# Chunks of 68, 60, 60 and 68 rows instead of four of 64, and the last store in two parts, in a DMA-bound matrix product

## The chip, the cores and the metric

The kernel runs on one core of a Trainium2 chip. The metric is the device time of one execution, in microseconds (us). Every execution also has a record of its span, from the core's first to its last instruction.

Ratios of two kernels are the mean time of one kernel's runs over that of the other's runs of the same rounds on the same chip, with a 95% interval. They are therefore not quite the ratio of the medians that are quoted beside them.

## The reference

```python
def reference(x, W, lora_A, lora_B, lora_E, scale):
    x_flat = x.reshape(-1, 256)                 # x: 16 x 2048 x 256, so 32768 rows of 1 KB
    y = x_flat @ W                              # W: 256 x 256
    lora_out = ((x_flat @ lora_A) * lora_E) @ lora_B    # rank 16
    return (y + scale * lora_out).reshape(16, 2048, 256)
```

All of it is float32. 33.55 MB are read and 33.55 MB are written. The kernel folds the low-rank part into one bfloat16 weight of 256 x 256, so each row needs one multiplication.

## The kernel before

The 32,768 rows are cut into four chunks of 64 rows per partition. Partition `p` of chunk `c` holds 64 consecutive rows, so neighbouring partitions lie 64 KB apart in memory. Three chunks fit in SBUF, the core's own memory (the "homes"); results overwrite their inputs and are stored from there; chunk 3 takes the home of chunk 0 once that is stored. One queue, on the sync engine (SP), issues all loads and stores in this order:

```python
ROWS = 64
N_CHUNKS = 4
N_HOMES = 3
ORDER = [                    # L: load, S: store; chunk, first row, last row
    ("A",),
    ("L", 0, 0, 8), ("L", 0, 8, 24), ("L", 0, 24, 40), ("L", 0, 40, 64),
    ("L", 1, 0, 32), ("L", 1, 32, 64),
    ("L", 2, 0, 16), ("L", 2, 16, 64),
    ("S", 0, 0, 40), ("S", 0, 40, 64),
    ("L", 3, 0, 32), ("L", 3, 32, 64),
    ("S", 1, 0, 64), ("S", 2, 0, 64), ("S", 3, 0, 64),
]                            # (set here with several entries to a line)
HELD = (2, 16)
HOLDERS = (("S", 0, 0, 40),)
# ... cut ...
    x_chunks = x_flat.rearrange("(c p b) k -> c p b k", p=P, b=ROWS)
    y_chunks = out_flat.rearrange("(c p b) m -> c p b m", p=P, b=ROWS)
# ... cut: in sync_program, for each entry (kind, c, s, e) of ORDER ...
            if kind == "L":
                for st in stored:
                    if st[1] == c - N_HOMES and st[2] < e and s < st[3]:
                        sync.wait_ge(stored[st], 16)
                ins = sync.dma_start(out=at_home, in_=x_chunks[c, :, s:e, :]).then_inc(loaded[op], 16)
            else:
                sync.wait_ge(s_done, ends.index((c * ROWS + e) // CG - 1) + 1)
                sync.dma_start(out=y_chunks[c, :, s:e, :], in_=at_home).then_inc(stored.get(op, stored_rest), 16)
```

Rows are computed in 64 groups of four rows per partition. The cast to bfloat16 is on POOL (GpSimd), the transposes and multiplications on PE (TensorE; PEld is its loading of weights), one copy on DVE (VectorE) and the copy of the result back to its home on ACT (ScalarE). POOL is held at row 16 of chunk 2 until the first store has landed.

## Time and profile before

| | before |
|---|---|
| time, median of 3 runs | 161.51 us (161.44 to 161.85) |
| execution whose profile is shown here | span 161.5 us, time 162.84 us |
| DMA queue of loads and stores, share of 16 engines' span | 97.2% |
| last instruction that computes ends | 118.6 us |

These lines are from the page of the kernel before: busy time (and share) of the engines; a row of 40 equal slices, each digit the busy share of the mean DMA engine in tenths; the DMA queue of loads and stores, q1, and a small one named instruction, q14 (packets, MB, share of 16 engines); and the chain that ended last.

```profile
span 161.5 us, 2024 instructions
...
PE 95.4 (59%) x782; PEld 83.4 (52%) x782; DVE 45.4 (28%) x66; ACT 66.1 (41%) x65; POOL 66.9 (41%) x70
...
DMA  7999999999999997998999999799799799699690
...
q1 hardware_dynamic: 2304, 67.13, 97.2%
...
q14 instruction: 3, 0.02, 0.0%
...
DMA 36%; PE 34%; POOL 1%; ACT 1%; issue 0%; SPq 0%; ACTq 0%; POOLq 0%
```

The DMA engines hardly rest, and no other engine is near that. The chain's share of PE (34%) does not contradict it: the chain passes through the engine that released the last issue, and that store then stood in a queue behind others.

When the loads and stores were issued shows in SP's timeline of the kernel before (start, length of the piece in us, operation, count):

```profile
0.43 4.95 SPq L148 DMA_DIRECT2D home<-in_x_dram  x8
27.66 9.87 SPq L153 DMA_DIRECT2D out_dram<-home  x2
75.94 7.69 SPq L148 DMA_DIRECT2D home<-in_x_dram  x2
83.68 35.34 SPq L153 DMA_DIRECT2D out_dram<-home  x3
```

The last store is issued by 119 us; queued stores keep the engines busy for 42 us more.

Two stretches of the kernel before, by windows (columns: from and to, length, busy time of PE, PEld, DVE, ACT and POOL, granted clock, DMA share, GB/s):

```profile
24.00:40.00 16.00, 14.52 (x134) 13.29 (x133) 7.61 (x11) 11.10 (x11) 11.78 (x12) 1.00 0.99 428
50.00:66.00 16.00, 10.96 (x101) 9.94 (x98) 5.87 (x9) 9.33 (x10) 6.97 (x7) 0.95 0.98 403
```

From 50 to 66 us the engines move less although they are as busy. Here the first store follows the loads of chunks 0 to 2.

Finally, the trace has a record of each DMA packet: start, duration, size. One packet is one partition's piece of one transfer, so each transfer is 128 packets, eight to an engine. The records do not name the engine; packets are chained here by the start of one falling on the end of another, within a few ns. The "excess" of a packet is its duration less that of the fastest packet of its size in the same trace.

```
packets of the kernel before (from the trace's records)
size B    count   fastest us   median us   longest us
 8192      128      0.309        0.309       0.754
49152      128      1.815        1.820       2.718
65536      384      2.418        2.418       2.625
excess summed over all packets, divided by 16 engines: 1.58 us
  of it in packets starting at  0 to 16 us: 0.49    56 to 64 us: 0.83    96 to 104 us: 0.09
one engine, eight packets in a row from 100.68 to 121.21 us: 2.516 to 2.625 us each instead of 2.418
```

### The profile page before, as it was taken

Reading aid. Unit: us, or ns where it says so; the run is one execution under the profiler, and the core shown is the slowest. Engines: PE = TensorE matmul, PEld = TensorE weight load, DVE = VectorE, ACT = ScalarE, POOL = GpSimd, SP = SyncE. Lnnn points to the kernel's source line nnn. Section 1 sums busy time; section 2 is a strip of 40 time slices with the busy share of each in tenths; the row PEclk is TensorE's granted clock in tenths of the full one; section 3 lists DMA queues with packets and bytes.
Section 4 is the critical chain, followed back from the end, with each engine's and each line's share of the span. In section 5 each row is a group of like instructions: output and inputs, shape, how many; then the busy total and the mean of one; then the engine's idle time right before and its main releaser. Section 6 shows DMA issues by size and latency. Waiting matters only on the chain.

```text
span 161.5 us, 2024 instructions
## 1 busy us (share of the span) xinstructions
PE 95.4 (59%) x782; PEld 83.4 (52%) x782; DVE 45.4 (28%) x66; ACT 66.1 (41%) x65; POOL 66.9 (41%) x70
## 2 busy tenths in 40 slices
PE   2988999969999990000899999999910000000000
PEld 1347999959999990000789989999900000000000
DVE  0141555535555550000155555555400000000000
ACT  3003677747777772000157777777730000000000
POOL 1516768577778840001578777788200000000000
PEclk9975999999999999555599999999996555555555
DMA  7999999999999997998999999799799799699690
GB/s 253 405 438 452 402 452 446 446 406 446 394 548 414 402 390 337 477 467 371 420 459 440 406 446 536 319 519 471 308 503 487 308 503 503 292 503 503 292 519 16
DMA packets 2515, 67.43 MB, mean 418 GB/s; under 512 B 448, under 2 KB 464, under 8 KB 592
## 3 DMA queue, kind: packets, MB, share of 16 engines
q1 hardware_dynamic: 2304, 67.13, 97.2%
q10 hardware_dynamic: 208, 0.28, 0.6%
q14 instruction: 3, 0.02, 0.0%
HBM read 33.85 MB, written 33.55 MB: 417 GB/s over the span
## 4 chain that ended last, share of the span: by engine, by line
DMA 36%; PE 34%; POOL 1%; ACT 1%; issue 0%; SPq 0%; ACTq 0%; POOLq 0%
DMA out_dram<-home 30%; PE psum_y L237 22%; PE psum_xt L226 12%; DMA home<-in_x_dram 6%; POOL stage L177 1%; ACT home L193 1%; ACTq L195 0%; SPq L308 0%; POOLq L176 0%; SPq L272 0%
## 5 line engine op out<-in xcount | busy, mean ns | idle before, releaser
L193 ACT COPY home<-psum_y 128x1024 f32<-128x1024 f32 x64 | 64.8, 1012 | 50.5 <-PE psum_y L237 50.5
L177 POOL CAST stage<-home 128x1024 bf16<-128x1024 f32 x64 | 66.2, 1042 | 44.8 <-DMA out_dram<-home 17.5
L237 PE MATMUL psum_y<-weff,xt 128*128 128x256 bf16 x512 | 69.6, 281 | 0.0
L210 DVE COPY xt<-psum_xt 128x1024 bf16<-128x1024 bf16 x64 | 44.3, 692 | 63.4 <-PE psum_xt L226 63.4
L237 PEld LDWEIGHTS psum_y<-weff,xt 128*128 128x128 bf16 x512 | 51.8, 101 | 6.5
L226 PE MATMUL psum_xt<-ident,stage 128*128 128x128 f32 x260 | 41.4, 283 | 19.3 <-POOL stage L177 19.0
L226 PEld LDWEIGHTS psum_xt<-ident,stage 128*128 128x128 f32 x260 | 31.5, 146 | 22.1 <-issue 20.7
L250 PE MATMUL psum_y<-ident 128*128 128x512 f32 x4 | 3.7, 1078 | 2.9 <-POOL ident L158 2.9
L250 PEld LDWEIGHTS psum_y<-ident 128*128 128x128 f32 x4 | 1.2, 324 | 3.9 <-POOL ident L158 2.9
L200 DVE TENSOR_SCALAR ate<-psum_y,e_sb 16x256 f32<-16x256 f32 x1 | 0.5, 472 | 6.9 <-PE psum_y L253 6.9
L193 ACT ACT_TABLE_LOAD x1 | 1.3, 1283 | 2.1 <-SPq L272 2.1
L259 PE MATMUL psum_y<-b_sb,ate 16*128 16x256 f32 x4 | 1.1, 400 | 0.0
L156 POOL MEMSET ident<- 128x128 f32 x1 | 0.2, 205 | 1.7 <-SPq L272 1.7
L253 PEld LDWEIGHTS psum_y<-ident,a_sb 128*16 128x16 f32 x2 | 0.2, 114 | 1.2 <-issue 1.2
L214 DVE TENSOR_TENSOR weff<-w_sb,psum_y 128x512 bf16<-128x512 f32 x1 | 0.7, 687 | 0.4 <-PE psum_y L259 0.4
L259 PEld LDWEIGHTS psum_y<-b_sb,ate 16*128 16x128 f32 x4 | 0.7, 184 | 0.2 <-issue 0.2
L158 POOL TENSOR_SCALAR_AFFINE_SELECT ident<-ident 128x128 f32<-128x128 f32 x1 | 0.3, 293 | 0.2 <-POOL ident L156 0.2
L253 PE MATMUL psum_y<-ident,a_sb 128*16 128x128 f32 x2 | 0.4, 273 | 0.0
L294 POOL MEMSET const-float32-0.0<- 128x1 f32 x1 | 0.1, 99 | 0.2 <-issue 0.2
L294 POOL MEMSET const-bfloat16-1.0<- 128x1 bf16 x1 | 0.1, 103 | 0.0
L294 POOL MEMSET const-uint8-127<- 128x1 uint8 x1 | 0.1, 103 | 0.0
L294 POOL MEMSET const-float32-1.0<- 128x1 f32 x1 | 0.1, 99 | 0.0
## 6 DMA issues: line engine op xcount, KB each, us to landing
home<-in_x_dram SPq DMA_DIRECT2D x4, 4096.0 KB, 25.1
home<-in_x_dram SPq DMA_DIRECT2D x3, 2048.0 KB, 13.8
home<-in_x_dram SPq DMA_DIRECT2D x1, 6144.0 KB, 58.9
out_dram<-home SPq DMA_DIRECT2D x1, 5120.0 KB, 48.3
home<-in_x_dram SPq DMA_DIRECT2D x1, 3072.0 KB, 20.7
out_dram<-home SPq DMA_DIRECT2D x1, 3072.0 KB, 46.0
home<-in_x_dram SPq DMA_DIRECT2D x1, 1024.0 KB, 5.4
w_sb<-in_W_dram ACTq DMA_DIRECT2D x1, 256.0 KB, 3.0
```

What stands on the lines that cost most here:

```text
L158: gpsimd.affine_select(out=ident[:], in_=ident[:], compare_op=ALU.not_equal, fill=1.0, base=0, pattern=[[-1, P]], channel_multiplier=1,).t ...
L177: gpsimd.tensor_copy(out=stage[g % NS][:], in_=home(c)[:, b:b + CG, :]).then_inc(s_stage[g % UNROLL], 1)
L193: scalar.copy(out=home(c)[:, b:b + CG, :], in_=psum_y[g % NY][:]).then_inc(s_free[(g + NY) % UNROLL], 1)
L200: vector.tensor_scalar(out=ate[:], in0=psum_y[0][:R, :KT, :P], scalar1=e_sb[:], scalar2=float(scale), op0=ALU.mult, op1=ALU.mult,).then_in ...
L210: vector.tensor_copy(out=xt[g % NX][:], in_=psum_xt[g % NT][:].bitcast(BF16)).then_inc(s_xt[g % UNROLL], 1)
L214: vector.tensor_add(out=weff[:], in0=w_sb[:], in1=psum_y[1][:, :KT, :]).then_inc(s_free[0], 1)
L226: ins = tensor.transpose(psum_xt[i % NT][:, b, :], words[:, b, :], ident[:])
L237: ins = tensor.matmul(psum_y[i % NY][:, b, :], xt[i % NX][:, b, t::KT], weff[:, t, :], start=(t == 0), stop=(t == KT - 1),)
L250: tensor.matmul(psum_y[1][:, :2, :], ident[:], ident[:, None, :].to_broadcast([P, 4, P]), start=True, stop=True)
L253: ins = tensor.transpose(psum_y[0][:R, t, :P], a_sb[:, t, :], ident[:])
L259: ins = tensor.matmul(psum_y[1][:, t, :], ate[:, t, :], b_sb[:], start=True, stop=True)
L294: nc = _bacc.Bacc("TRN2", target_bir_lowering=False, num_devices=1)
```

## The change

The intent is in its few words: partitions 68 or 60 KB apart instead of a power of two. The home of chunk 0 gets 68 rows, and those of chunks 1 and 2 get 60, so that SBUF holds them as before and chunk 3 (68 rows) can take chunk 0's home. The last store is cut in two. The core of the diff, with cuts marked:

```diff
-ROWS = 64
-N_CHUNKS = 4
+ROWS = (68, 60, 60, 68)
+START = (0, 68, 128, 188)
...
-    ("L", 0, 40, 64),
-    ("L", 1, 0, 32),
-    ("L", 1, 32, 64),
+    ("L", 0, 40, 68),
+    ("L", 1, 0, 28),
+    ("L", 1, 28, 60),
     ("L", 2, 0, 16),
-    ("L", 2, 16, 64),
+    ("L", 2, 16, 60),
     ("S", 0, 0, 40),
-    ("S", 0, 40, 64),
-    ("L", 3, 0, 32),
-    ("L", 3, 32, 64),
-    ("S", 1, 0, 64),
-    ("S", 2, 0, 64),
-    ("S", 3, 0, 64),
+    ("S", 0, 40, 68),
+    ("L", 3, 0, 36),
+    ("L", 3, 36, 68),
+    ("S", 1, 0, 60),
+    ("S", 2, 0, 60),
+    ("S", 3, 0, 36),
+    ("S", 3, 36, 68),
...
-    x_chunks = x_flat.rearrange("(c p b) k -> c p b k", p=P, b=ROWS)
-    y_chunks = out_flat.rearrange("(c p b) m -> c p b m", p=P, b=ROWS)
+    def in_chunks(rows):
+        return [
+            rows[P * s:P * (s + n), :].rearrange("(p b) k -> p b k", b=n) for s, n in zip(START, ROWS)
+        ]
...
-    homes = [sbuf(f"home{h}", [P, ROWS, K], FP32) for h in range(N_HOMES)]
+    homes = [sbuf(f"home{h}", [P, ROWS[h], K], FP32) for h in range(N_HOMES)]
```

The rest renames indices. The number of groups and the instructions on PE, DVE, ACT and POOL do not change.

More of the change, by code (lines that the diff above doesn't have):

```diff
@@ L42 @@
 CG = 4
-GPC = ROWS // CG
-N_GROUPS = N_CHUNKS * GPC
+N_GROUPS = sum(ROWS) // CG
+PLACES = [(c, b) for c, rows in enumerate(ROWS) for b in range(0, rows, CG)]
 NS, NX, NT, NY = 2, 2, 2, 2
@@ L69 @@
     KT = K // P
-    assert N == N_CHUNKS * ROWS * P and K == M and KT == 2
-    x_chunks = x_flat.rearrange("(c p b) k -> c p b k", p=P, b=ROWS)
-    y_chunks = out_flat.rearrange("(c p b) m -> c p b m", p=P, b=ROWS)
+    assert N == sum(ROWS) * P and K == M and KT == 2
+    def in_chunks(rows):
+        return [
+            rows[P * s:P * (s + n), :].rearrange("(p b) k -> p b k", b=n) for s, n in zip(START, ROWS)
+        ]
+    x_chunks, y_chunks = in_chunks(x_flat), in_chunks(out_flat)
     sbuf, psum, sem = nc.alloc_sbuf_tensor, nc.alloc_psum_tensor, tc.alloc_semaphore
-    homes = [sbuf(f"home{h}", [P, ROWS, K], FP32) for h in range(N_HOMES)]
+    homes = [sbuf(f"home{h}", [P, ROWS[h], K], FP32) for h in range(N_HOMES)]
     stage = [sbuf(f"stage{i}", [P, CG, K], BF16) for i in range(NS)]
@@ L94 @@
         for op in ORDER
-        if op[0] == "S" and (op in HOLDERS or op[1] < N_CHUNKS - N_HOMES)
+        if op[0] == "S" and (op in HOLDERS or op[1] < len(ROWS) - N_HOMES)
     }
@@ L99 @@
     n_rest = sum(op[0] == "S" and op not in waited for op in ORDER)
-    ends = sorted((c * ROWS + e) // CG - 1 for kind, c, s, e in (op for op in ORDER if op[0] == "S"))
+    ends = sorted((START[c] + e) // CG - 1 for kind, c, s, e in (op for op in ORDER if op[0] == "S"))
     s_ident = sem("ident_made")
@@ L147, in sync_program @@
                         sync.wait_ge(stored[st], 16)
-                ins = sync.dma_start(out=at_home, in_=x_chunks[c, :, s:e, :]).then_inc(loaded[op], 16)
+                ins = sync.dma_start(out=at_home, in_=x_chunks[c][:, s:e, :]).then_inc(loaded[op], 16)
                 if n == 1:
@@ L151, in sync_program @@
             else:
-                sync.wait_ge(s_done, ends.index((c * ROWS + e) // CG - 1) + 1)
-                sync.dma_start(out=y_chunks[c, :, s:e, :], in_=at_home).then_inc(stored.get(op, stored_rest), 16)
+                sync.wait_ge(s_done, ends.index((START[c] + e) // CG - 1) + 1)
+                sync.dma_start(out=y_chunks[c][:, s:e, :], in_=at_home).then_inc(stored.get(op, stored_rest), 16)
     def gpsimd_program():
@@ L167, in gpsimd_program @@
         for g in range(N_GROUPS):
-            c, b = g // GPC, g % GPC * CG
+            c, b = PLACES[g]
             for op, landed in loaded.items():
@@ L190, in scalar_program @@
         for g in range(N_GROUPS):
-            c, b = g // GPC, g % GPC * CG
+            c, b = PLACES[g]
             scalar.wait_ge(s_y, g + 1)
```

## The prediction

> **What bounds the kernel now.** The DMA engines. The queue table gives the queue of loads and stores 97.2% of the 16 engines' span; the 40 slices show it busy from first to last. PE is busy 59%, ACT and POOL 41%. After 118.6 us no engine computes: queued stores drain for 42 us. The chain of waits passes through the first store (48.3 us from issue to landing), but it arrives there only because that transfer stood in the queue.
>
> **Is memory slow at a 64 KB pitch?** The change assumes so. The packet records of the trace have one packet for each partition row. Of the 384 packets of 65,536 bytes the median took 2.418 us, the fastest 2.418 too: 27.1 bytes/ns per engine, 434 GB/s for 16. Packets of 40,960 bytes took 1.514 us, of 8,192 bytes 0.309 us: about 0.008 us plus bytes/27.2 per ns. That is all but the fabric ceiling of 435 GB/s of the Trainium skill, "DMA: Bandwidth & Descriptors", section "Where 436 GB/s comes from". So nearly every packet runs at the engine's own rate. The same page ("Latency and other measured facts") reports slow HBM copies at row pitches of 512 KiB and more and a cure by a few KiB of padding; 64 KB is below its range, and this trace shows no standing loss.
>
> **What is left to gain.** All packets at their fastest sum to 155.1 us per engine; the first bulk packet starts at 2.1 us, and 0.4 us follow the last. So the floor is about 157.7 us, 2.4% below 161.5. Lost are, per engine: about 0.5 us of stretched packets in the first 9 us; 0.8 us at about 59 to 62 us, where each engine's last load packet before the first store is stretched (49,152 bytes in about 2.6 us, not 1.82); small gaps. One engine loses 1.2 us more: its eight packets of the store of chunk 1 took about 2.57 us instead of 2.418. It ends at 161.07 us; the others end between 158.3 and 159.9. Transfers are bound to engines by partition, so nothing rebalances that.
>
> **What the change does.** Bytes are the same. Packets per engine rise from 120 to 128 of bulk size: 0.06 us. Groups (64) and instructions on PE, DVE, ACT, POOL stay. Chunk 0's four more rows put about 1.2 us more work before the end of the loads, but fewer rows precede the first store, so POOL's held group starts about 1.2 us earlier; compute still ends some 40 us before the stores. While the loads of chunk 3 wait for the first store, 28 rows (8.5 us) of the second are queued: no starvation. The split last store lets its first part be issued earlier, but about 20 us of slack made that worthless already; its smaller packets do not rebalance engines.
>
> So only the stretched packets can change: they might shrink if they come from rows 64 KB apart meeting in the memory's channels. I believe half of it: some of the slowest engine's 1.2 us and of the opening's 0.5 us goes; the read-to-write turn stays.
>
> **Prediction.** 160.7 us (ratio 0.995), 8 in 10 between 159.2 and 162.0. Faster by over 2%: 0.04; within 2%: 0.92; slower by over 2%: 0.04.
>
> **What would show it.** Right: bulk packets still at 27.1 bytes/ns, DMA share about 97%, average about 420 GB/s, computing over by about 118 us, and the difference in the end of the slowest engine. If pitch matters more, the stretch at 59 to 62 us and the straggler both vanish and the span nears 158.5.
>
> **What would make it wrong.** A pitch of 68 or 60 KB that slows steady packets; a straggler that comes back elsewhere (no gain); an idle stretch of DMA at 75 to 85 us; both stretches due to 64 KB, giving 2% and over.

## More of the kernel before

What POOL waited for in the kernel before (us in total, times, longest):

```profile
POOL stage L177 <- DMA out_dram<-home: 17.5, 1, 17.5
POOL stage L177 <- PE psum_xt L226: 16.1, 49, 1.5
POOL stage L177 <- DMA home<-in_x_dram: 11.2, 5, 3.5
```

## The result, and the profile after

| | before | after |
|---|---|---|
| time, median of 6 runs | 161.47 us (161.40 to 161.85) | 161.78 us (161.48 to 162.34) |
| ratio | | 1.0019 (0.9999 to 1.004) |
| profiled execution | span 161.5, time 162.84 us | span 160.5, time 161.82 us |

The time is the same. The two profiles, however, differ by 1.0 us of span in favour of the changed kernel. The third row resolves that: span and time are not one scale. In the 126 executions of all the kernels for which both were recorded, the time was 1.28 to 1.38 us above the span (about 1.33 in the middle; these spans are rounded to 0.1 us). A typical execution of before, at 161.5 us, therefore has a span of about 160.2. The profile that was read was of one that took 1.3 us longer.

The page of the changed kernel, the same lines:

```profile
span 160.5 us, 2026 instructions
...
PE 93.9 (59%) x782; PEld 82.5 (51%) x782; DVE 45.4 (28%) x66; ACT 66.1 (41%) x65; POOL 66.8 (42%) x70
...
DMA  6999999999999999999999999979998999799994
...
q1 hardware_dynamic: 2448, 67.13, 97.8%
...
q14 instruction: 3, 0.02, 0.0%
...
DMA 54%; PE 17%; POOL 1%; ACT 1%; SPq 0%; issue 0%; ACTq 0%
```

The queue has 144 packets more: the 128 of one more transfer, and its 16 completions. The chain that ended last now runs through the DMA engines for 54% of the span where it was 36%. That is another path through the same full queue, not a change of the limit: the DMA share is 97 to 98% in both.

SP's timeline of the changed kernel:

```profile
0.43 5.02 SPq L153 DMA_DIRECT2D home<-in_x_dram  x8
28.09 9.51 SPq L158 DMA_DIRECT2D out_dram<-home  x2
73.79 8.91 SPq L153 DMA_DIRECT2D home<-in_x_dram  x2
82.74 38.72 SPq L158 DMA_DIRECT2D out_dram<-home  x4
```

The same two windows of the changed kernel:

```profile
24.00:40.00 16.00, 14.52 (x133) 13.56 (x134) 7.61 (x11) 10.12 (x10) 13.12 (x13) 1.00 1.00 430
50.00:66.00 16.00, 9.73 (x90) 8.80 (x87) 5.26 (x8) 8.40 (x9) 6.01 (x6) 0.96 0.98 400
```

The loss at the first store (50 to 66 us) is all there: 400 GB/s, after 403.

What POOL waited for in the changed kernel:

```profile
POOL stage L182 <- DMA out_dram<-home: 16.5, 1, 16.5
POOL stage L182 <- DMA home<-in_x_dram: 16.4, 7, 4.6
POOL stage L182 <- PE psum_xt L231: 14.5, 45, 1.4
```

POOL's hold ends sooner (73.8 us instead of 75.9), but then it finishes chunk 2 before the first load of chunk 3, now of 36 rows, has landed, and waits 4.6 us for it. ACT's last copy, which started at 117.61 us in the kernel before, starts at 120.06. This costs nothing, since the engines reach the last store only at 148.7 us.

The packet records of the changed kernel:

```
size B    count   fastest us   median us   longest us
 8192      128      0.307        0.309       0.502
45056      128      1.665        1.669       2.747
61440      256      2.267        2.267       2.459
excess summed over all packets, divided by 16 engines: 1.52 us (before: 1.58)
  of it in packets starting at  0 to 16 us: 0.37    56 to 64 us: 0.93    96 to 104 us: 0.04
one engine, nine packets in a row from about 102 to 123.6 us: 2.35 to 2.46 us each instead of 2.267
```

A packet of 61,440 bytes at 2.267 us is 27.1 bytes/ns, the rate of a packet of 65,536 bytes at 2.418 us before. The stretch at the first store is as large as before. The one slow engine is back, in the same place, slower by the same 6%.

### The profile page after: what moved, and what is told of

Read it like the earlier page. It is cut to its first block, busy times and chain, and to the rows that moved or that the text cites. A ratio compares the mean times of both kernels' runs of the same rounds, so it can differ in the third digit from the quotient of the medians.

```text
span 160.5 us, 2026 instructions
## 1 busy us (share of the span) xinstructions
PE 93.9 (59%) x782; PEld 82.5 (51%) x782; DVE 45.4 (28%) x66; ACT 66.1 (41%) x65; POOL 66.8 (42%) x70
## 3 DMA queue, kind: packets, MB, share of 16 engines
q1 hardware_dynamic: 2448, 67.13, 97.8%
## 4 chain that ended last, share of the span: by engine, by line
DMA 54%; PE 17%; POOL 1%; ACT 1%; SPq 0%; issue 0%; ACTq 0%
DMA out_dram<-home 28%; DMA home<-in_x_dram 25%; PE psum_y L242 11%; PE psum_xt L231 6%; POOL stage L182 1%; ACT home L198 1%; SPq L153 0%; ACTq L200 0%; SPq L313 0%; SPq L277 0%
## 5 line engine op out<-in xcount | busy, mean ns | idle before, releaser
L242 PE MATMUL psum_y<-weff,xt 128*128 128x256 bf16 x512 | 68.5, 278 | 0.0
L242 PEld LDWEIGHTS psum_y<-weff,xt 128*128 128x128 bf16 x512 | 51.1, 100 | 6.0
L231 PE MATMUL psum_xt<-ident,stage 128*128 128x128 f32 x260 | 40.6, 280 | 23.2 <-POOL stage L182 22.7
```

The lines of the kernel that those rows point to most:

```text
L231: ins = tensor.transpose(psum_xt[i % NT][:, b, :], words[:, b, :], ident[:])
L242: ins = tensor.matmul(psum_y[i % NY][:, b, :], xt[i % NX][:, b, t::KT], weff[:, t, :], start=(t == 0), stop=(t == KT - 1),)
```

## Experiments

Fourteen kernels were run, each beside the kernel before on the same chip. Those that are meant to give the reference's result were all found correct; those that give a wrong one say so.

### 1. The kernel before, again

No edit.

> The kernel before, unchanged, once more, to see what one profile is worth. The changed kernel's profiled span was 160.5 us beside a run time of 161.82; the profile of before that the prediction rested on had a span of 161.5 us beside a run time of 162.84, although its timed runs took 161.4 to 161.85. Theory A (the first profile of before fell on an unusually long execution, and a span is about 1.3 us shorter than the time): the new span is 160.0 to 160.6 us, the time about 161.5, and the slowest DMA engine ends near 160 us instead of 161.07. Theory B (161.5 us is the usual span of before, and the change did shorten the work of the engines by 1 us but lost it outside the span): the new span is again 161.3 to 161.7. The ratio is that of a kernel with itself: 1.000, within 0.002.

Measured: 161.52 us (161.36 to 162.87), ratio to the other runs of itself 0.9982 (0.9938 to 1.0026). The profiled execution:

```profile
span 160.4 us, 2024 instructions
...
q1 hardware_dynamic: 2304, 67.13, 98.0%
...
q14 instruction: 3, 0.02, 0.0%
```

Theory A holds. In this profile the span is 160.4 us with a time of 161.71, and the slowest engine ends at 159.89 us instead of 161.07. The stretch at 56 to 64 us (1.02 us per engine) and the slow engine (about 2.57 us a packet) are both there, so they belong to ordinary executions. What made the first profile's execution long is then visible in its packet records, read again with the packets chained backwards from the end:

```
kernel before, first profile                 first store from   last load ends   end of engine
engine with eight slow packets (of 2.52 to 2.63)   61.94 us        100.68 us       159.85 us
engine that ended last (no slow packet of 65,536)  63.49 us        103.11 us       161.07 us
```

They are two engines, not one. The slow engine ended at 159.85 us there and at 159.89 here. The engine that ended last had been stretched twice before the first store: two packets of 49,152 bytes in succession, from 58.36 to 63.49 us, took 2.471 and 2.669 us instead of 1.815. It then met a short halt near 86.5 us (0.30 us without a packet of loads or stores, then one packet 0.54 us too long). The sum checks: its last packet of the first two stores ended at 82.855; 16 load packets of 1.213 and a halt of 0.84 give 103.1.

The trace shows what filled those 0.30 us: a packet of 8,192 bytes of the queue q14, by its name a fetch of instructions, from 86.49 us for 0.309 us. The other two of q14's packets, at 80.95 and 102.70 us, lie in such gaps as well. Every one of the twelve traces with computing has three of them within the span, and the four without (experiments 5, 12, 13 and 14) have none. In eleven of the twelve, the packet after the second of them took 0.38 to 0.62 us too long (in experiment 8 the chain is not certain there); why is not known. Whether this costs the execution anything depends on which engine is struck.

The 11 executions of before beside this one ran from 161.43 to 162.96, four of them above 162. A single profile of this kernel is worth about 1 us either way.

### 2 and 3. Each part of the change alone

Pitch alone: the changed kernel with the last store whole.

```diff
-    ("S", 3, 0, 36),
-    ("S", 3, 36, 68),
+    ("S", 3, 0, 68),
```

> The chunks of 68, 60, 60 and 68 rows, the last store in one piece. Theory P (the row pitch costs time, and the changed pitch gains some, which the split store gives back): faster than before by 0.3% to 1%. Theory N (neither pitch nor split acts on the time): ratio 0.999 to 1.003, like the whole change at 1.0019; the stretched packets at about 60 us and the one slow engine in the store of chunk 1 both stay.

Split alone: the kernel before with the last store in two.

```diff
-    ("S", 3, 0, 64),
+    ("S", 3, 0, 32),
+    ("S", 3, 32, 64),
```

> Four chunks of 64 rows, the last store in two parts of 32 rows. Theory P: slower than before by 0.2% to 0.5%, since the split would have to cost what the pitch gained. Theory N: ratio 0.999 to 1.002; eight packets more per engine at about 0.008 us each are 0.06 us.

Measured: pitch alone 161.75 us (161.56 to 162.78), ratio 0.9992 (0.9951 to 1.0033). Split alone 161.61 us (161.39 to 162.38), ratio 0.9982 (0.9943 to 1.002). Both are theory N (the second lies just below its range of 0.999 to 1.002, with an interval that covers it): no gain of either part is seen, nor one that the other takes back. A side finding of the pitch-alone trace is that the last store's 69,632 bytes per partition did not travel as one packet. They went as two of 34,816. The number of packets is therefore the same with and without the change's own split. Whether that was the reason for the split is not known.

### 4. The dose: partitions 256 KB apart

```diff
-    x_chunks = x_flat.rearrange("(c p b) k -> c p b k", p=P, b=ROWS)
-    y_chunks = out_flat.rearrange("(c p b) m -> c p b m", p=P, b=ROWS)
+    x_chunks = x_flat.rearrange("(p c b) k -> c p b k", p=P, b=ROWS)
+    y_chunks = out_flat.rearrange("(p c b) m -> c p b m", p=P, b=ROWS)
```

> The dose: everything as before, but partition p holds the 256 consecutive rows from 256p, so that partitions lie 256 KB apart in memory instead of 64, in loads and stores. Theory P: a larger power of two is worse; bulk packets lengthen, at least 1% slower, more of them stretched at the opening and at about 60 us. Theory N: median packets of 65,536 bytes stay at 2.418 us and the ratio is 0.998 to 1.003.

Measured: 162.41 us (162.11 to 163.85), ratio 1.0042 (0.9996 to 1.0088). The median packet of 65,536 bytes took 2.418 us, as before, so a pitch four times as large does not slow steady transfers. The time is between the theories and its interval touches zero effect; experiment 14 comes back to it.

### 5. The transfers without the computing

Each store waits for the loads of its rows, and the programs of POOL, DVE, PE and ACT's copies are left out. The result is x, wrong.

```diff
-                sync.wait_ge(s_done, ends.index((c * ROWS + e) // CG - 1) + 1)
+                for ld in loaded:
+                    if ld[1] == c and ld[2] < e and s < ld[3]:
+                        sync.wait_ge(loaded[ld], 16)
...
+        for name in set_up_loaded:
+            sync.wait_ge(set_up_loaded[name], 16)
...
-        for g in range(N_GROUPS):       # ACT's copies
+        for g in range(0):
...
-        gpsimd_program()
         scalar_program()
-        vector_program()
-        tensor_program()
```

(Without the second part of this edit, nothing ordered the set-up loads before the end.)

> The kernel before with its computing taken out: the same loads and stores in the same order, each store waiting for the loads of its rows alone. The result is x itself, wrong on purpose. Theory C (the engine that is slow by about 0.15 us a packet between 100 and 121 us is slowed by computing that runs beside stores): no such engine, and the slowest engine ends at about 159.2 us or earlier instead of 159.9; time 0.3 to 1 us less. Theory A (it is an address or row effect): the slow engine stays. The stretch of about 0.8 us per engine at the first turn from loads to stores stays under both; if it goes, it too came from computing. If the ratio is 0.995 or more, the whole time is transfers, and no computing is left to remove.

Measured: 160.78 us (160.70 to 160.97), ratio 0.9931 (0.988 to 0.9983). The slow engine is gone: of the 384 packets of 65,536 bytes one is 0.11 us over the fastest, and none of the others is over it by as much as 0.06. The slowest engine ends at 158.97 us. The stretch at the first store stays (0.99 us per engine). So the slow engine comes with computing, the stretch does not, and computing in all costs about 0.7% of the time (0.2% to 1.2% by the interval). The page lists two queues only; q14 is missing:

```profile
span 159.4 us, 79 instructions
...
q1 hardware_dynamic: 2304, 67.13, 98.3%
q10 hardware_dynamic: 208, 0.28, 0.5%
```

### 6. One small store early

```diff
     ("L", 1, 0, 32),
+    ("S", 0, 0, 8),
     ("L", 1, 32, 64),
...
-    ("S", 0, 0, 40),
+    ("S", 0, 8, 40),
...
-HOLDERS = (("S", 0, 0, 40),)
+HOLDERS = (("S", 0, 8, 40),)
```

> The kernel before, but the first 8 rows of chunk 0 are stored on their own, in the queue between the two loads of chunk 1 (near 31 us). Theory F (the stretch belongs to the first store of the execution): it moves to about 31 us, and the turn at about 60 us loses it; ratio about 1.000. Theory T (it belongs to each turn from a long run of loads to stores): a second stretch, at about 31 us, and 0.3% to 0.6% slower. Theory P, that the pitch causes it, has no place for either.

Measured: 162.13 us (161.71 to 163.24), ratio 1.0021 (0.9976 to 1.0067). The windows of this kernel, to be held against those of the kernel before above:

```profile
24.00:40.00 16.00, 13.02 (x103) 11.40 (x104) 5.64 (x9) 7.63 (x8) 9.03 (x10) 0.89 1.00 393
50.00:66.00 16.00, 13.03 (x120) 11.85 (x118) 6.92 (x10) 11.11 (x11) 8.49 (x9) 1.00 0.98 426
```

The dip moved with the store: 393 GB/s at 24 to 40 us and 426 at 50 to 66, where the kernel before had 428 and 403. In the packet records the excess at 24 to 32 us is 1.34 us per engine and at 56 to 64 us it is 0.00, although loads turn into stores there as before. Of the theories, F alone fits: the stretch came with the first store of the execution and not again at the later turn. It was moved, not removed, and the time did not fall. This is one trace, and experiment 9 will not fit as well.

### 7. The last store issued early

The store of chunk 3 waits for its loads, and ACT puts the results of chunk 3 elsewhere. Chunk 3 of the result is x, wrong.

```diff
-                sync.wait_ge(s_done, ends.index((c * ROWS + e) // CG - 1) + 1)
+                if c < N_CHUNKS - 1:
+                    sync.wait_ge(s_done, ends.index((c * ROWS + e) // CG - 1) + 1)
+                else:
+                    for ld in loaded:
+                        if ld[1] == c:
+                            sync.wait_ge(loaded[ld], 16)
...
-            scalar.copy(out=home(c)[:, b:b + CG, :], in_=psum_y[g % NY][:]) ...
+            to = home(c)[:, b:b + CG, :] if c < N_CHUNKS - 1 else scratch[g % 2][:]
+            scalar.copy(out=to, in_=psum_y[g % NY][:]) ...
```

(`scratch` is two buffers of 8-bit numbers. One bfloat16 buffer was refused for a race between ACT's own writes.)

> The kernel before, but the store of chunk 3 waits for its loads instead of its results, and ScalarE puts chunk 3's results into a small scratch as 8-bit numbers; so all stores are issued by about 103 us while computing runs on to about 118 us. Chunk 3 of the result is x, wrong on purpose. Theory C (computing beside stores slows one engine): the slow packets last until about 120 us as before. Theory S (they belong to the time in which the issuing queue still waits to issue a store): they end at about 105 us. Time within 0.3% of before under either.

Measured: 161.51 us (161.32 to 161.88), ratio 0.9977 (0.9924 to 1.0029). All stores were issued by 102.2 us, while ACT computed on (from SP's and ACT's timelines):

```profile
82.55 19.68 SPq L159 DMA_DIRECT2D out_dram<-home  x3
116.72 1.01 ACT L200 CAST scratch<-psum_y 128x1024 uint8<-128x1024 f32 x1 [0.30 <-PE psum_y L244]
```

The slow engine's packets went on until 121.0 us, as in the kernel before. Of the two theories C holds: they follow the computing, not the state of the issuing queue. They do not end with it at once, however. In eleven of the twelve traces with computing, the last packet of the slow row starts 0.02 to 1.9 us after ACT's last copy has ended (in the twelfth, the first profile of before, 0.05 us ahead of that), and it is still 0.06 to 0.22 us too long. What slows the engine thus outlasts the computing a little; "beside computing" is not exact.

### 8. No hold on POOL

```diff
-HOLDERS = (("S", 0, 0, 40),)
+HOLDERS = ()
```

> The kernel before without the wait that holds the casting engine at row 16 of chunk 2 until the first store has landed; so computing of chunk 2 runs beside the first stores (61 to 82 us) and less is left for later. The result is right. Theory C: one engine has packets of the first store of about 1.6 us instead of 1.514 while computing runs there, and the slow packets after 100 us end earlier, at about 113 us. Theory A: the first stores stay clean. Time: within 0.4% of before.

Measured: 162.27 us (162.11 to 162.65), ratio 1.0021 (0.9981 to 1.0061). One chain of packets of the first store, from 66.2 to 74.2 us, took 1.60 to 1.62 us each instead of 1.514: again 6%, and now in the first store, beside which computing runs. That much is theory C. The other half of the expectation was wrong: computing did not end earlier (the last copy starts at 117.11 us; it still had to follow the loads of chunk 3), so the slow packets after 100 us went on to 121.9 us.

### 9 and 10. A first write at the very start

If the stretch belongs to the first write, a small write at the start might take it where the engines have little to do. Both kernels get one copy more, 16 rows from x to the output, one per 2,048 rows, overwritten later; number 9 is the kernel before with it, number 10 the changed kernel with it.

```diff
     def scalar_program():
+        ins = scalar.dma_start(
+            out=out_flat.rearrange("(q r) m -> q r m", q=16)[:, 0, :],
+            in_=x_flat.rearrange("(q r) k -> q r k", q=16)[:, 0, :],
+        ).then_inc(s_touched, 16)
+        opening.append(ins.ins.name)
...
+                if not touched:                # before the first store
+                    sync.wait_ge(s_touched, 16)
+                    touched = True
```

> The kernel before, with one small copy more: at the very start, before the first bulk load, ScalarE's queue copies 16 rows of x, one per DMA engine and 2,048 rows apart, to the output, where the later stores overwrite them; the first store waits for it. Theory F (the stretch of about 0.8 us per engine belongs to the first write to the output, whichever rows): the packets at 57 to 62 us are no longer stretched, the opening is longer by 0 to 0.8 us since some of the stall falls into the idle time before 2 us, and the time is 0.1% to 0.5% less. Theory F2 (it belongs to the first write of each region of the output, so these 16 rows do not cover it): the stretch at 60 us stays and the time is the same.

> The changed kernel (68, 60, 60, 68 rows, last store in two parts) with the same small copy at the start. If pitch and split act on nothing, it stands to the kernel with that copy and 64-row chunks as the change stood to before: within 0.3%, not faster by more than 0.2%. If the pitch does gain something that the first-store stall hid, this one is the faster of the two by 0.3% or more.

Measured: number 9 162.24 us (161.70 to 163.07), ratio 1.0027 (0.9994 to 1.0061); number 10 162.81 us (161.75 to 163.07), ratio 1.0046 (1.0014 to 1.0079). The hoped-for gain failed in both. The stretch at 56 to 64 us fell to 0.03 us per engine in number 10 but only to 0.62 in number 9. In both traces most engines have gaps near 5 us, of up to 1.3 us in number 9 and 1.7 in number 10; in the other traces a few engines at most have one there, of up to 0.6 us. So the early copy costs at the start at least what it saves. Why number 9 kept most of its stretch is open; each rests on one trace. Neither of the two theories fits both traces, so "the first write takes the stretch" is not shown; what stands is that the stretch moved in experiment 6. The changed kernel was not the faster of the two (its ratio is 1.0019 times that of number 9, as the change stood to before), so no gain of the pitch is seen behind the stall either. No version that computes the right result was faster than the kernel before with an interval clear of 1.

### 11. More, shorter multiplications

```diff
-                    ins = tensor.matmul(
-                        psum_y[i % NY][:, b, :], xt[i % NX][:, b, t::KT], weff[:, t, :], ...
+                    for h in range(2):
+                        ins = tensor.matmul(
+                            psum_y[i % NY][:, b, h * P:(h + 1) * P], xt[i % NX][:, b, t::KT],
+                            weff[:, t, h * P:(h + 1) * P], ...
```

> The kernel before with each of the 512 multiplications done as two of half the columns, so that TensorE issues about half as many instructions again per group; the result is right. If the slow engine's packets are slowed in proportion to the number of instructions running (their fetches, events or records), they take clearly more than 2.57 us, 2.62 or above; if by the data that the other engines move, they stay at 2.57 or fall, since groups come no faster.

162.15 us, correct. The window from 100 to 118 us of the kernel before, in experiment 1:

```profile
100.00:118.00 18.00, 17.31 (x159) 15.86 (x156) 8.44 (x13) 13.83 (x15) 10.94 (x11) 1.00 1.06 456
```

In the same columns, the kernel with more multiplications:

```profile
100.00:118.00 18.00, 17.82 (x268) 17.49 (x265) 8.58 (x13) 13.48 (x15) 11.08 (x11) 1.00 1.05 454
```

The instructions in the window rise from 354 to 572 (sums of the counts), while DVE, ACT and POOL do the same work. The slow engine's first six packets of that store took on average 0.22 us more than 2.418, where they took 0.15 in experiment 1. Its delay thus grew with the number of instructions that run, 1.46 times for 1.62 times as many, and not with the data of the other three engines. That is one trace to a kernel, but in the other traces with computing such packets are 0.12 to 0.18 us too long. Fetches of instructions, as far as the trace records them, do not fit: in both windows q14 has one packet (at 103.12 and 103.02 us), in a gap of another engine. (The kernel with more multiplications has one packet of 16,384 bytes on a further queue of that name, at 124.81 us, after the slow row.) The events of the instructions, or the writing of the very records that the profile is made of, would fit, also with a slow packet after computing has ended. Every execution here was recorded, so no run tells these apart; the cause of the slow engine stays open below the level "comes with computing".

### 12, 13 and 14. The transfers alone, at three pitches

The same edit as in experiment 5, made to the kernel before (12), to the changed kernel (13) and to the kernel of experiment 4 (14); the result is x, wrong. They were run because whole kernels scatter too much between executions to settle a few tenths of a microsecond.

> The transfers of before alone, without computing, once more (result x, wrong on purpose), as the yardstick for the two runs beside it: such a kernel's four times before lay within 0.3 us (160.70 to 160.97), where those with computing scatter over 1 to 2 us. Expected 160.7 to 161.0 us.

> The transfers of the changed kernel alone (68, 60, 60, 68 rows, last store in two parts; result x, wrong on purpose). Theory P (some of the stretched packets come from rows a power of two apart): at least 0.4 us less than the 64-row transfers of the same call. Theory N (pitch of 60 to 68 KB acts on nothing): within 0.15 us of them, probably some 0.06 us more for the eight extra packets per engine; the stretch at about 60 us is as long as in the 64-row transfers.

> The transfers alone with partitions 256 KB apart (result x, wrong on purpose). With computing, 256 KB measured 0.42% above before, with an interval that touched zero. If that was real and lies in the memory, this is 0.4 to 0.9 us above the 64-row transfers of the same call; if it was scatter or needs computing, within 0.15 us.

| transfers alone | median of 6, us | range, us | ratio to the whole kernel before |
|---|---|---|---|
| 64 KB (12) | 160.71 | 160.41 to 161.36 | 0.9948 (0.9912 to 0.9983) |
| 68 and 60 KB, last store split (13) | 161.17 | 160.70 to 162.36 | 0.9982 (0.9939 to 1.0026) |
| 256 KB (14) | 161.68 | 161.26 to 163.07 | 1.0024 (0.9977 to 1.0071) |

The changed transfers are not faster than the 64 KB ones; their median is 0.46 us slower, with overlapping ranges. A gain of 0.4 us and more, which theory P required, is ruled out as far as six runs can do it. That they are slower is not shown. Theory N's own expectation, within 0.15 us, was missed as well: these executions scatter more than the four before. So was that of an equal stretch at the first store (0.84 us per engine against 0.56, one trace each; with computing it scatters as much). The 256 KB transfers are slower by 0.97 us in the median (expected were 0.4 to 0.9 if the effect was real), and all but one of the six 64 KB executions were faster than the fastest of them. The 0.42% of experiment 4 was thus probably real. It does not lie in steady packets. In the traces it shows at the second turn from loads to stores, at 96 to 104 us: 0.48 us per engine in experiment 14 and 0.39 in experiment 4. In ten traces with a 64 KB pitch the figure is 0.01 to 0.23 (mean 0.08), in four with 60 and 68 KB 0.04 to 0.28 (mean 0.18). That is one trace to a kernel, so it is a hint of the place and no more.

## Why the prediction was wrong

The predicted time was 160.7 us; measured were 161.78, inside the range given, but the predicted gain of 0.8 us did not come: the interval of the ratio, 0.9999 to 1.004, excludes the predicted 0.995.

1. **The limit: right.** Loads and stores fill the DMA engines, bulk packets kept 27.1 bytes/ns, and the DMA share was 97.8% (predicted about 97%).
2. **The step that failed: "So only the stretched packets can change: they might shrink if they come from rows 64 KB apart meeting in the memory's channels. I believe half of it".** No gain of it was found. Of its two named parts, the slow engine stayed at the changed pitch (2.41 us a packet on average instead of 2.267, the same 6%); it goes when computing goes (experiment 5), lasts until computing is over and about a packet longer (7), and moves to where computing runs (8). The opening's stretch (packets starting before 16 us) scatters from 0.08 to 0.50 us per engine between traces that all have a 64 KB pitch and no write in that time, and from 0.17 to 0.50 at the changed pitch, so its fall from 0.49 to 0.37 says nothing. The third stretch, at 59 to 62 us, which the prediction rightly left out of its gain, moved with the first store of the execution (6; what makes it is open, 9). The transfers alone show no gain of 0.4 us or more at the changed pitch (13).
3. **The term that was mis-sized.** The prediction read 161.5 us twice, as the span of the profile and as the time, and took them for the same. They were not: that execution took 162.84 us, and spans are 1.3 us below times. So the room above its floor was too large. The floor of 157.7 us is a span; as a time it is 157.7 + 1.3 = 159.0 us, 1.5% below 161.5 and not 2.4%. It also gave the slow engine an end that was another's: "One engine loses 1.2 us more ... It ends at 161.07 us". The 1.2 us are right, but that engine ended at 159.85; the end at 161.07 was of another engine, delayed twice at the first store and once by a packet of q14. In experiment 1 the slow engine is the last, at 159.89 us, and others end at 159.54 and 159.51. Taking its delay away entirely would have shortened that execution by some 0.35 us, not 1.2.

4. **Of what the split does: right.** It did nothing (experiment 3). Of the pitch the prediction named the alternative "a straggler that comes back elsewhere (no gain)"; it came back in the same place.
5. **"Computing over by about 118 us": wrong, at no cost.** POOL did start again earlier, but ran into the later first load of chunk 3; the last copy ended at 121.07 us. Slack hid it.
6. **What it took from the Trainium skill.** The ceiling of 435 GB/s in "DMA: Bandwidth & Descriptors", section "Where 436 GB/s comes from", agrees with 434 GB/s from the packets here. The entry on row pitch in the section "Latency and other measured facts" of that page starts at 512 KiB, and there it has 207 GB/s, close to the 214 that it calls full. The prediction rightly noted that 64 KB lies below its range, and still gave the idea half a chance. The trace of before spoke against it: one would look for a conflict between rows that lie a fixed distance apart in steady packets first, and their median was their fastest. That alone does not prove it, since the 256 KB pitch kept that median too and still cost time (14); the measured ratio and experiment 13 decide it.

## What to carry to other kernels

When the median packet of a DMA-bound kernel already takes as long as its fastest, a new memory layout has nothing to speed up in the steady transfers (it can still cost time elsewhere, as 256 KB did). Before crediting a layout with the stretched packets that remain, find out what they coincide with (here the first store of the execution, the time in which other engines compute, and packets of another queue). Compare span with span and time with time, and profile the unchanged kernel twice: two profiles of the same kernel differed here by 1.1 us, more than the whole predicted gain. The removal of one engine's delay is worth only its lag behind the next slowest engine, not the delay itself.

## What the Trainium skill lacked or had wrong

- "DMA: Bandwidth & Descriptors", section "Latency and other measured facts": the entry on HBM row pitch covers copies from HBM to HBM from 512 KiB up. Between HBM and SBUF, pitches of 60 to 68 KB and of 64 KB gave the same steady rate (27.1 bytes/ns per engine). At 256 KB the packets kept that rate as well (2.418 us for 65,536 bytes), yet the transfers alone took 161.68 us instead of 160.71.
- No page has the stall of the first store: each engine's last load packets before it were stretched by 0.56 to 1.15 us in sum per engine in all traces whose first store came at about 60 us with no earlier write, and by 1.34 us where the packets of a small store came at about 33 us. A small early copy left 0.62 us of it in one trace and 0.03 in another.
- No page ties a slow DMA engine to computing: here one engine's stores ran about 6% slower while other engines computed and for about a packet after that (2.57 us instead of 2.418 for 65,536 bytes), and the delay grew from 0.15 to 0.22 us a packet when the instructions in 18 us rose from 354 to 572.
- No page has what a packet of the instruction queue costs a DMA engine that is full: 0.31 us each, three to an execution, and in eleven of twelve traces, once, 0.38 to 0.62 us more on the packet that follows.
- "Perfetto Trace Analysis", section "Summary: the profiler window per engine type", mentions a gap of about 6.2 us between the profile's total time and the reported execution time. The pair of measures here, span and device time, differs by about 1.33 us (1.28 to 1.38 in 126 executions), so such a gap has to be measured for the pair at hand.
